# Modulation rows of gate_a, shift_f and scale_f: two weight tiles scaled and summed ahead of one TensorE pass

## Chip, cores and metric

The kernel runs on one core of one Trainium2 chip. The metric is device time in microseconds (us), the median of several executions; lower is better.

## What is computed

Two transformer blocks run one after the other on 256 tokens of width 2048, in float32. The part that matters here is the modulation of the first block: one vector `c` of 2048 numbers becomes six vectors of 2048.

```
mod = silu(c) @ w_ada[l] + b_ada[l]            # w_ada: 2048 x 12288
shift_a, scale_a, gate_a, shift_f, scale_f, gate_f = split(mod, 6)
h = rms_norm(x, g_attn_pre) * (1 + scale_a) + shift_a
proj = h @ w_in                                 # then two kinds of attention
x = x + gate_a * rms_norm(concat(diff_out, dsa_out) @ w_o, g_attn_post)
h = rms_norm(x, g_ffn_pre) * (1 + scale_f) + shift_f
x = x + gate_f * rms_norm((silu(h @ w_gate) * (h @ w_up)) @ w_down, g_ffn_post)
```

The second block (latent attention and a gated convolution) follows and has nothing of this modulation.

## The kernel before

Every engine has one queue, executed in the order in which the program emits. A driver in Python, `run`, writes that order out by hand. Its input is a list of steps. A matmul step takes a unit of 2 x 128 rows of a weight matrix by up to 512 columns. Each unit is split first: ScalarE copies it to a rounded part `wh` (L286), VectorE subtracts to get the rest `wl` (L287), and TensorE then multiplies high by high, low by high and high by low (three matmuls `mm` for each 128 rows and 128 tokens). Splits are emitted up to three units ahead of the matmuls (`LOOK = 3`), into four buffers each (`N_SPLIT = 4`).

Weights arrive as tiles of 128 x 2048 numbers (1 MB) in a ring of four buffers `raw`, and two or three more (`rawb`) lent from other storage. SyncE (SP) issues their transfers in the order of the list, each when a buffer has been released.

A modulation step (`ada`) has a tile of its own in the same ring: 128 rows of `w_ada` by the 2048 columns of one of the six vectors. Before, `ada_full` gives each tile straight to TensorE: a column of silu(c), repeated to 32 columns, is the stationary side, and four float32 products of 512 columns go side by side to four strips of 32 columns of the array, summed in one PSUM bank over 16 tiles. The trace shows eight instructions for the four products. After the sixteenth tile a finishing generator is spawned: `col_fin` for shift_f and scale_f, `row_fin` for gate_a.

The 32 steps of gate_a and shift_f are merged evenly among the matmul steps of the second part of w_in (`sd`), the 16 steps of scale_f among those of the first half of w_o (`so1`). Both attentions run in the background of these steps as generators (`idx_gen`, `dsa_gen`, `diff_gen`): each yields a time, and the driver resumes it when its own clock, which counts matmul columns, has passed it. `softmax_stage` does the row maximum on VectorE (L871) and the exponentials on ScalarE (L877), VectorE scales the result (L927, L989, L990), and TensorE transposes it (`tp<-ident,p`). `gate_f` comes later and keeps `ada_full`; of its tiles eleven are already scaled and summed by VectorE into `adacc` (L660).

Of the kernel before, what the change touches and what calls it, by code (L numbers as in the profile page):

```python
# [9 lines left out]
F32 = mybir.dt.float32  # L10
# [3 lines left out]
AF = mybir.ActivationFunctionType  # L14
OP = mybir.AluOpType
AX = mybir.AxisListType

P = 128
D = 2048
# [20 lines left out]
def kernel(ctx: ExitStack, tc: tile.TileContext, a, freq, out):  # L40
    nc = tc.nc
# [13 lines left out]
    V, A, G = nc.vector, nc.scalar, nc.gpsimd  # L55
# [15 lines left out]

    T = PE

    # ------------------------------------------------------------------ storage
    slots = deque(range(14))
    slot_of = {}

# [8 lines left out]
    def free(*names):  # L86
        for n in names:
            slots.append(slot_of.pop(n))
# [30 lines left out]
    def sc_bank():  # L119
        return psx.tile([P, 512], F32, name="sc", tag="sc", bufs=2)  # L120

    # ------------------------------------------------------------------ driver
    bg = []
    H = {}

# [9 lines left out]
    def spawn(gen, name=None):  # L135
        h = Handle()
        if name is not None:
            H[name] = h
        e = [gen, clock["t"], h]
        if step_gen(e):  # L140
            bg.append(e)
        return h
# [73 lines left out]
    def release(it):  # L216
        ring.append(it["res"])
        lend(lent["max"])

    def run(steps):  # L220
# [74 lines left out]
        for s in steps:  # L295
            if s["kind"] == "call":
                s["fn"]()
                continue
            if s["kind"] == "ada":
                s["item"]["use"](s["item"]["tile"])  # L300
                s["item"]["left"] = 0
                release(s["item"])
                s["after"]()
                pump_dma()
                pump_split(max(0, first_open))
                tick()
                continue
            u, ts = s["unit"], s["ts"]
            g = u["grp"]
            if g.need is not None:  # L310
                names = [x for t in ts for x in g.need(u["kcs"], t)]
                if not done(*names):
                    require(names, g.name)
                    keep_warm(g, ts[0])
            while pos["split"] <= u["idx"]:
                n0 = pos["split"]
                pump_dma()
                pump_split(u["idx"])
                assert pos["split"] > n0, g.name
            for i, kc in enumerate(u["kcs"]):  # L320
                for t in ts:
                    if t not in g.ps:
                        g.ps[t] = mm_bank()
                    hi, lo = g.lhs(kc, t)
                    o = g.ps[t][:, :g.n]
                    fs, ls = kc == g.kcs[0], kc == g.kcs[-1]
                    T.matmul(o, hi, u["wh"][:, i, :g.n], start=fs, stop=False)
                    T.matmul(o, hi, u["wl"][:, i, :g.n], start=False, stop=False)
                    T.matmul(o, lo, u["wh"][:, i, :g.n], start=False, stop=ls)
                if i + 1 < len(u["kcs"]):  # L330
                    tick()
            if s["fin"]:
                unit_done[u["idx"]] = True
                while first_open < len(units) and unit_done[first_open]:
                    first_open += 1
            pump_split(u["idx"])
            for t in s["ends"]:
                spawn(g.post(t, g.ps[t][:, :g.n]), f"{g.name}.{t}")
            tick()
# [9 lines left out]
    def merge(xs, ys, frac=1.0):  # L349
        res, j = [], 0  # L350
        nx = max(1, int(frac * len([x for x in xs if x["kind"] == "mm"])))
        i = 0
        for x in xs:
            res.append(x)
            if x["kind"] == "mm":
                i += 1
                while j < len(ys) and (j + 1) * nx <= i * len(ys) + 0:
                    res.append(ys[j])
                    j += 1
        res += ys[j:]  # L360
        return res

# [9 lines left out]
                t = tt  # L372
            stages[-j](items[i])

    # ------------------------------------------------------------------ constants
    v1 = wtile(tag="P", bufs=4, name="v1")
    v1 = v1[:, :P]
    rows = lambda v, n: v.rearrange("o (r c) -> (o r) c", c=P)[:n]
# [125 lines left out]
        V.tensor_scalar(nlam, nlam, 0.2, None, op0=OP.subtract)  # L504


    # ------------------------------------------------------------------ helpers
    def rstd_of(ssq, n, width, name="rstd"):
        k = ssq.shape[1]
        v = small(k, name + "v")  # L510
# [41 lines left out]
            A.activation(h, src, AF.Copy, scale=scale)  # L552
            V.scalar_tensor_tensor(l, src, scale, h, op0=OP.mult, op1=OP.subtract)

    # ------------------------------------------------------------------ modulation
    def ada_item(load, use, after=lambda: None):
        return {"kind": "ada", "item": {"kind": "ada", "load": load, "use": use}, "after": after}

# [41 lines left out]
    def ada_chunk_fin(ci, ps):  # L600
        k0, nk = CH[ci]
        w = nk * P
        sb = wtile(name="adasb")
        A.activation(sb[:, :w], ps[:, :w], AF.Copy)
        yield 3.0
        pb = quad_transpose(sb[:, :w])
        c2_ = small(16, "c2")
        c2 = c2_[:, :2 * nk].rearrange("p (k g) -> p k g", g=2)
        V.tensor_copy(c2, pb[:, :, 0:64:32])
        V.tensor_add(c2, c2, pb[:, :, 64:P:32])  # L610
        V.scalar_tensor_tensor(Acol[:, k0:k0 + nk], c2[:, :, 1], 1.0, col1[:, 64 + k0:64 + k0 + nk],
                               op0=OP.add, op1=OP.add)
        V.tensor_mul(Acol[:, k0:k0 + nk], Acol[:, k0:k0 + nk], col1[:, 16 + k0:16 + k0 + nk])
        V.tensor_add(tcol[:, k0:k0 + nk], c2[:, :, 0], col1[:, 48 + k0:48 + k0 + nk])
        if k0 == 8:
            while len(slots) < 2:
                yield 0.5
            hid["hi"][1], hid["lo"][1] = big("h1h1", dt=R32), big("h1l1", dt=R32)
        for kc in range(k0, k0 + nk, 2):
            tl, j = nT[kc // 8], kc % 8  # L620
            h = hid["hi"][kc // 8][:, j:j + 2, :]
            for d in range(2):
                A.activation(h[:, d, :], tl[:, j + d, :], AF.Identity, scale=Acol[:, kc + d:kc + d + 1],
                             bias=tcol[:, kc + d:kc + d + 1])
                V.tensor_scalar(tl[:, j + d, :], tl[:, j + d, :], Acol[:, kc + d:kc + d + 1],
                                tcol[:, kc + d:kc + d + 1], op0=OP.mult, op1=OP.add)
            V.tensor_sub(hid["lo"][kc // 8][:, j:j + 2, :], tl[:, j:j + 2, :], h)  # L627
            mark(f"h.{kc}")
            yield 0
        if ci == 2:  # L630
            free("nT0")
        if ci == 4:
            free("nT1")

    def ada_full(which, fin, engs="P" * 16):
        st = {}
# [39 lines left out]
    def col_fin(dst, boff, scale_g=None):  # L676
        def gen(ps):
            sb = wtile(name="adasb")
            A.activation(sb, ps, AF.Copy)
            yield 4.13  # L680
            pb = quad_transpose(sb)
            d = dst.rearrange("p (j b) -> p b j", b=4)
            V.tensor_copy(d, pb[:, :, 0:P:32])
            V.tensor_add(dst, dst, col1[:, boff:boff + 16])
            if scale_g is not None:
                V.scalar_tensor_tensor(dst, dst, 1.0, col1[:, scale_g:scale_g + 16], op0=OP.add,
                                       op1=OP.mult)
        return gen
# [28 lines left out]
                set_state("ada_free", True)  # L717
        return gen

    # ------------------------------------------------------------------ first norm  # L720
    ssx = cst.tile([P, 2, 4], F32, name="ssx")
    first = ada_chunk(0)
    firsts = []
# [25 lines left out]
    free("x0", "x1", "ada0", "ada1", "ada2", "ada3")  # L749
    hid["hi"], hid["lo"] = [big("h1h0", dt=R32), None], [big("h1l0", dt=R32), None]  # L750

    # ------------------------------------------------------------------ w_in of the first block
    acc = {}
    for q in range(2):
        acc["A", q] = big(f"accA{q}", (P, 2, 2, 512))
# [39 lines left out]
            s += g.steps()  # L795
        return s

    # index scores and the selection of keys
    iws = cst.tile([P, 2, 16], F32, name="iws")

    def idx_gen():
# [301 lines left out]
    steps.insert(len(steps) - 8, call(lambda: lend(2)))  # L1103
    steps.append(call(start_idx))
    steps += win_groups(S_G, range(12, 16), False, "c4") + [call(start_dsa)]
    gate_a = ada_full(2, row_fin("Ga", 2, "g_attn_post"))
    shift_f = ada_full(3, col_fin(tfcol, 80))
    scale_f = ada_full(4, col_fin(Afcol, 96, 32))
    gate_f = ada_full(5, row_fin("Gf", 5, "g_ffn_post"), "PPPPPVVVVVVVVVVV")
    sd = win_groups(D_G, range(4, 16), False, "d")  # L1110
    nd = [i for i, x in enumerate(sd) if x["unit"]["grp"].c0 == 1536][0]
    sd.insert(nd, call(start_diff))
    steps += merge(sd, gate_a + shift_f)

    # ------------------------------------------------------------------ output of the attention
    mix_hi = lambda kc, t: (hid["mh%d" % (kc // 8)][:, kc % 8, t * P:(t + 1) * P],
                            hid["ml%d" % (kc // 8)][:, kc % 8, t * P:(t + 1) * P])
    w_o = a["w_o"][0]
# [91 lines left out]
    def after_o():  # L1210
        free("mh0", "ml0", "mh1", "ml1")

    # ------------------------------------------------------------------ feed-forward
    DFF = 5632
    w_gate, w_up, w_down = a["w_gate"][0], a["w_up"][0], a["w_down"][0]
    lhs2 = lambda kc, t: hilo_lhs(*hid["h2"])(kc, t)
# [103 lines left out]

    steps += fsteps[nf:]

    # ------------------------------------------------------------------ second block
    w_in2 = a["w_in_2"]
    lhs3 = lambda kc, t: hilo_lhs(*hid["h3"])(kc, t)
    need3 = lambda ks, t: [f"h3.{t}.{k // 4}" for k in ks]
# [58 lines left out]
    steps += Grp("ck0", w_in2, 512, 288, range(16), lhs3, post_ck0).steps()  # L1385
    steps += Grp("ck1", w_in2, 800, 288, range(16), lhs3, post_ck1).steps()

    # gated convolution
    C_IN, B_GATE, C_GATE, Z_CONV = 3136, 5184, 7232, 9280
    G_MLA, G_CONV, Z_MLA = 11328, 13376, 1088  # L1390
    uT = {}
# [75 lines left out]
        steps += Grp(f"oconv{g}", a["w_o_conv_2"], 512 * g, 512, range(16), lhs_y, post_oconv(g),  # L1467
                     need=lambda ks, t: [f"bgate{k // 4}.{t}" for k in ks]).steps()

    # latent attention  # L1470
    knT, vt, qnT = [None, None], [None, None], [None, None]

    def kv_alloc():
# [199 lines left out]
    for g in range(4):  # L1673
        steps += Grp(f"omla{g}", a["w_o_mla_2"], 512 * g, 512, range(16), lhs_att, post_omla(g)).steps()

    # output projection
    ot = [None, None]
    x2 = [None, None]
    ssz = cst.tile([P, 2, 4], F32, name="ssz")
# [72 lines left out]
```

## Time and profile before

| | |
|---|---|
| median of 3 runs | 2367.16 us (2366.83 to 2367.84) |
| span of the profiled execution | 2365.9 us |
| its own time beside the span | not listed; the span lies 1.3 us below the median |
| TensorE busy | 2315.8 us, 98% |
| VectorE busy | 1306.1 us, 55% |
| ScalarE busy | 1069.0 us, 45% |
| modulation tiles of gate_a, shift_f, scale_f | 48, used by TensorE from 228.85 to 482 us |

The span goes from the first to the last instruction. PE is TensorE, PEld its weight load, DVE is VectorE, ACT ScalarE, POOL GpSimd, SP SyncE. Matmuls overlap in the records, so a matmul's own duration is longer than the distance from its start to the start of the next one, and it is that distance which counts.

### The profile page before, as it was taken

The page shows a single profiled execution, that of the slowest core. Times are in us where ns is not written, and L with a number is a line of the kernel's source. Part 1 is how long each engine was busy: PE and PEld are TensorE (multiplying, and loading weights), DVE is VectorE, ACT ScalarE, POOL GpSimd, SP SyncE. Part 2 cuts the span into 40 slices and gives each one's busy share as a digit, 9 for nine tenths or more (in the row PEclk, how much of TensorE's full clock was granted, in tenths as well). Part 3 has the DMA queues.
Part 4 walks back from the last instruction along what each step waited for, and adds up shares of the span by engine and source line. Part 5 has one row for each costly group of instructions (what it writes and reads, how often), then busy time and mean ns, then how long its engine had stood idle before and what let it go on. Part 6 is the DMA issues. An engine that isn't in the chain of part 4 may idle for free.

```text
span 2365.9 us, 27898 instructions
## 1 busy us (share of the span) xinstructions
PE 2315.8 (98%) x11044; PEld 1842.3 (78%) x11044; DVE 1306.1 (55%) x1710; ACT 1069.0 (45%) x1503; POOL 96.8 (4%) x117
## 2 busy tenths in 40 slices
PE   7999999999999999999998999999999999999998
PEld 5666666677887888888887888888888988888887
DVE  3656756556664444554556655555544654554554
ACT  4434345546444444434444644444445544444443
POOL 1311011010000000000001000000000000000000
PEclk9999999999999999999999999999999999999999
DMA  9996888957775556556554665565565553565563
GB/s 302 330 320 237 318 309 301 318 209 277 242 261 191 191 192 195 179 196 195 186 188 144 220 195 190 179 200 188 179 204 161 168 171 125 172 219 196 187 204 125
DMA packets 237619, 506.57 MB, mean 214 GB/s; under 512 B 9288, under 2 KB 31984, under 8 KB 228400
## 3 DMA queue, kind: packets, MB, share of 16 engines
q1 hardware_dynamic: 235392, 496.14, 62.3%
q0 software_dynamic: 1872, 8.58, 1.1%
q8 instruction: 86, 1.41, 0.2%
q14 instruction: 45, 0.37, 0.0%
q10 hardware_dynamic: 224, 0.07, 0.0%
HBM read 500.56 MB, written 4.19 MB: 213 GB/s over the span
## 4 chain that ended last, share of the span: by engine, by line
PE 75%; DVE 1%; ACT 1%; issue 1%; POOL 0%; DVEq 0%; POOLq 0%; ACTq 0%
PE mm L65 71%; PE tp L70 1%; PE sc L65 1%; PE tp L65 1%; PE tpb L70 1%; DVE wl L287 0%; DVE xr L1155 0%; ACT h3h L1163 0%; DVE h3l L1166 0%; POOL rstd L513 0%; ACT wh L286 0%; ACT junk L1178 0%; DVE ot L1705 0%; ACT hm L1277 0%; DVE hm L1273 0%
## 5 line engine op out<-in xcount | busy, mean ns | idle before, releaser
L287 DVE TENSOR_TENSOR wl<-raw,wh 128x1024 fp32r<-128x1024 f32 (+3 forms) x723 | 871.9, 1212 | 766.5 <-ACT wh L286 760.4
L286 ACT ACTIVATE wh<-raw 128x1024 fp32r<-128x1024 f32 (+3 forms) x723 | 745.9, 1038 | 696.4 <-PE mm L65 686.3
L65 PE MATMUL mm<-wh,h3h 128*128 128x512 f32 (+1 forms) x992 | 387.1, 390 | 1.7 <-ACT h3h L1163 1.2
L65 PE MATMUL mm<-wl,h3h 128*128 128x512 f32 (+1 forms) x992 | 380.7, 384 | 0.4 <-DVE wl L287 0.4
L65 PE MATMUL mm<-wh,h3l 128*128 128x512 f32 (+1 forms) x992 | 381.0, 384 | 0.0
L65 PE MATMUL mm<-wh,h2h 128*128 128x512 f32 x704 | 276.3, 393 | 0.0
L65 PE MATMUL mm<-wl,h2h 128*128 128x512 f32 x704 | 274.6, 390 | 0.9 <-DVE wl L287 0.9
L65 PE MATMUL mm<-wh,h2l 128*128 128x512 f32 x704 | 274.7, 390 | 0.0
L65 PEld LDWEIGHTS mm<-wh,h3h 128*128 128x128 f32 x992 | 186.7, 188 | 37.8 <-ACT h3h L1163 1.6
L65 PEld LDWEIGHTS mm<-wh,h3l 128*128 128x128 f32 x992 | 186.5, 188 | 37.4 <-DVE h3l L1166 0.4
L65 PEld LDWEIGHTS mm<-wl,h3h 128*128 128x128 f32 x992 | 186.8, 188 | 34.8 <-DVE wl L287 0.6
L65 PE MATMUL mm<-wh,h1h 128*128 128x512 f32 (+2 forms) x384 | 154.0, 401 | 3.4 <-ACT wh L286 2.5
L65 PEld LDWEIGHTS mm<-wl,h2h 128*128 128x128 f32 x704 | 132.5, 188 | 28.1 <-DVE wl L287 1.2
L65 PEld LDWEIGHTS mm<-wh,h2h 128*128 128x128 f32 x704 | 132.5, 188 | 27.7 <-issue 0.8
L65 PEld LDWEIGHTS mm<-wh,h2l 128*128 128x128 f32 x704 | 132.4, 188 | 27.6
L65 PE MATMUL mm<-wl,h1h 128*128 128x512 f32 (+2 forms) x384 | 142.7, 372 | 7.8 <-DVE wl L287 7.8
L65 PE MATMUL mm<-wh,h1l 128*128 128x512 f32 (+2 forms) x384 | 142.0, 370 | 1.9 <-DVE h1l L627 1.9
L65 PE MATMUL mm<-wh,acth 128*128 128x512 f32 x352 | 139.3, 396 | 0.0
L65 PE MATMUL mm<-wh,actl 128*128 128x512 f32 x352 | 137.1, 390 | 0.0
L65 PE MATMUL mm<-wl,acth 128*128 128x512 f32 x352 | 137.0, 389 | 0.0
L65 PEld LDWEIGHTS mm<-wh,h1h 128*128 128x128 f32 x384 | 72.8, 190 | 55.7 <-issue 26.7
L65 PEld LDWEIGHTS mm<-wl,h1h 128*128 128x128 f32 x384 | 72.9, 190 | 21.2 <-DVE wl L287 10.9
(412 smaller groups left out, 2777.7 us busy)
## 6 DMA issues: line engine op xcount, KB each, us to landing
raw<-in_w_in_dram SPq DMA_DIRECT2D x134, 1024.0 KB, 5.2
raw<-in_w_ada_dram SPq DMA_DIRECT2D x47, 1024.0 KB, 4.9
raw<-in_w_gate_dram SPq DMA_DIRECT2D x44, 1024.0 KB, 5.3
raw<-in_w_up_dram SPq DMA_DIRECT2D x44, 1024.0 KB, 5.2
raw<-in_w_down_dram SPq DMA_DIRECT2D x44, 1024.0 KB, 5.1
raw<-in_w_ada_dram SPq DMA_DIRECT2D x36, 512.0 KB, 8.9
rawb<-in_w_ada_dram SPq DMA_DIRECT2D x17, 1024.0 KB, 6.5
raw<-in_w_o_conv_dram SPq DMA_DIRECT2D x16, 1024.0 KB, 5.1
```

What stands on the lines that cost most here:

```text
L65: return nc.tensor.matmul(o, l, r, **kw)
L70: return nc.tensor.transpose(o, i, idn)
L286: A.activation(wh[:, :m, :g.n], src, AF.Copy)
L287: V.tensor_sub(wl[:, :m, :g.n], src, wh[:, :m, :g.n])
```

## The change

A new function `ada_pairs` replaces `ada_full` for gate_a, shift_f and scale_f. The tiles of a vector are taken two by two. ScalarE multiplies the even tile in place by its column of silu(c), in two halves of 1024 columns. VectorE multiplies the odd tile by its own column and adds the even one, again in two halves, in place. Then the even buffer is released. A spawned generator waits 5.0 on the driver's clock, runs four products of the sum with a column of ones on TensorE, and releases the odd buffer. After the eighth pair it goes on to the same finish. `merge` places the odd step directly behind its even one, and `run` leaves the release to the generator.

```
+                if not s.get("keep"):
+                    release(s["item"])
...
+                    if ys[j - 1].get("keep") and j % 2:
+                        res.append(ys[j])
+                        j += 1
...
+    def ada_pairs(which, fin):
...
+        def rows(src, i):
+            if i == 0:
+                st["ps"] = psx.tile([P, 512], F32, name="ada", tag="ada")
+            for j in range(4):
+                T.matmul(st["ps"][32 * j:32 * j + 32, :], ones32, src[:, 512 * j:512 * (j + 1)],
+                         start=i == 0, stop=i == 7, tile_position=(0, 32 * j), skip_group_check=True)
+        def summed(i, item):
+            yield 5.0
+            rows(item["tile"], i)
+            release(item)
+            if i == 7:
+                yield from fin(st["ps"])
+        def even(kc):
+            def use(tl):
+                for j in range(2):
+                    s = slice(1024 * j, 1024 * (j + 1))
+                    A.activation(tl[:, s], tl[:, s], AF.Copy, scale=csil[:, kc:kc + 1])
+                st["one"] = first_item
...
+        def odd(kc):
+            def use(tl):
+                a = st["one"]["tile"]
+                for j in range(2):
+                    s = slice(1024 * j, 1024 * (j + 1))
+                    V.scalar_tensor_tensor(tl[:, s], tl[:, s], csil[:, kc:kc + 1], a[:, s], op0=OP.mult,
+                                           op1=OP.add)
+                release(st["one"])
+            def after():
+                spawn(summed(kc // 2, step["item"]), f"ada{which}" if kc == 15 else None)
...
-    gate_a = ada_full(2, row_fin("Ga", 2, "g_attn_post"))
-    shift_f = ada_full(3, col_fin(tfcol, 80))
-    scale_f = ada_full(4, col_fin(Afcol, 96, 32))
+    gate_a = ada_pairs(2, row_fin("Ga", 2, "g_attn_post"))
+    shift_f = ada_pairs(3, col_fin(tfcol, 80))
+    scale_f = ada_pairs(4, col_fin(Afcol, 96, 32))
```

## Rows read from the trace of the kernel before

**Rows 1.** The page, part 1: busy us, share of the span, instructions of each engine.
```profile
PE 2315.8 (98%) x11044; PEld 1842.3 (78%) x11044; DVE 1306.1 (55%) x1710; ACT 1069.0 (45%) x1503; POOL 96.8 (4%) x117
```
**Rows 2.** The page, part 4: chain that ended last, shares by engine.
```profile
PE 75%; DVE 1%; ACT 1%; issue 1%; POOL 0%; DVEq 0%; POOLq 0%; ACTq 0%
```
**Rows 3.** Instructions of tile ada, 228 to 482 us: count, duration ns min/median/max, starts.
```profile
L65 PE MATMUL ada<-raw,csil x248: 592/604/617, 228.8 to 473.2; 128*32 128x512 f32 x124
L65 PE MATMUL ada<-rawb,csil x136: 592/604/617, 249.3 to 481.6; 128*32 128x512 f32 x136
```
**Rows 4.** Timeline of PE around one modulation tile: start us, duration us, instruction.
```profile
270.64 0.39 PE L65 MATMUL mm<-wl,h1h 128*128 128x512 f32 x1
270.87 0.39 PE L65 MATMUL mm<-wh,h1l 128*128 128x512 f32 x1
271.19 1.06 PE L65 MATMUL ada<-rawb,csil 128*32 128x512 f32 x8
272.18 0.50 PE L65 MATMUL mm<-wh,h1h 128*128 128x512 f32 x1
272.52 0.39 PE L65 MATMUL mm<-wl,h1h 128*128 128x512 f32 x1
```
**Rows 5.** Windows of the stretch with the 48 tiles: busy us (instructions) of each engine.
```profile
228.00:287.00 59.00, 59.00 (x287) 35.73 (x285) 42.52 (x101) 25.33 (x39) 2.61 (x2) 1.00 0.79 293
287.00:330.00 43.00, 43.00 (x225) 27.75 (x228) 25.05 (x56) 17.61 (x46) 5.74 (x9) 1.00 0.90 326
330.00:400.00 70.00, 70.00 (x364) 43.06 (x356) 41.99 (x94) 33.54 (x78) 6.56 (x5) 1.00 0.83 304
400.00:482.00 82.00, 82.00 (x440) 51.30 (x436) 45.04 (x99) 40.43 (x82) 7.10 (x7) 1.00 0.91 327
sum 254.00, PE 254.00 PEld 157.84 DVE 154.60 ACT 116.91 POOL 22.01; mean PE 63.50 PEld 39.46 DVE 38.65 ACT 29.23 POOL 5.50
```
The columns behind the length are PE, PEld, DVE, ACT, POOL, granted clock, DMA share, GB/s.

**Rows 6.** Groups of ACT and DVE, 228 to 482 us; last, tile adacc by itself.
```profile
L286 ACT ACTIVATE wh<-raw 128x1024 fp32r<-128x1024 f32 x34 | 35.3, 1058 | 11.0 <-PE mm L65 9.2 <-DVE wl L287 1.4 <-DMA raw<-in_w_o_dram 0.2
L1041 ACT ACTIVATE mh<-tp,gdiff 128x512 fp32r<-128x512 f32 x4 | 2.7, 686 | 3.8 <-PE tp L70 3.8
L954 ACT ACTIVATE mh<-tp 128x512 fp32r<-128x512 f32 x4 | 2.4, 597 | 3.5 <-PE tp L65 3.5
L287 DVE TENSOR_TENSOR wl<-raw,wh 128x1024 fp32r<-128x1024 f32 x34 | 41.0, 1222 | 30.4 <-ACT wh L286 28.3 <-PE mm L65 2.1
L660 DVE SCALAR_TENSOR_TENSOR adacc<-raw,csil,adacc x10: 2342/2344/2346, 563.9 to 706.0; 128x2048 f32<-128x2048 f32 x10
```
**Rows 7.** Waits of PE, 210 to 500 us: total us, times, longest.
```profile
PE mm L65 <- DVE wl L287: 1.2, 1, 1.2
```
**Rows 8.** Timeline, all engines: the end of one softmax and its transpose.
```profile
447.10 0.48 DVE L990 SCALAR_TENSOR_TENSOR p<-p,rs 128x256 f32<-128x256 f32 x1
...
447.88 1.06 PE L65 MATMUL ada<-raw,csil 128*32 128x512 f32 x8
...
448.87 0.33 PE L70 MATMUL tp<-ident,p 128*128 128x128 f32 x1
```
**Rows 9.** Tenth gate_a tile: its issue, its use; then transfers of its kind, 230 to 400 us.
```profile
260.43 0.33 SPq L642 DMA_DIRECT2D rawb<-in_w_ada_dram  x1
...
280.43 1.06 PE L65 MATMUL ada<-rawb,csil 128*32 128x512 f32 x8
...
rawb<-in_w_ada_dram SPq DMA_DIRECT2D x11, 1024.0 KB, 7.0
```
**Rows 10.** Windows of two slices of 15 us, columns as in Rows 5.
```profile
270.00:285.00 15.00, 15.00 (x80) 8.99 (x78) 14.52 (x49) 4.00 (x5) 1.20 (x1) 1.00 0.89 344
285.00:300.00 15.00, 15.00 (x83) 9.40 (x76) 8.06 (x19) 2.73 (x3) 0.09 (x1) 1.00 1.02 401
```

More of the change, by code (lines that the diff above doesn't have):

```diff
@@ L301, in run @@
                 s["item"]["left"] = 0
-                release(s["item"])
+                if not s.get("keep"):
+                    release(s["item"])
                 s["after"]()
@@ L633, in ada_chunk_fin, with load_of, load @@
             free("nT1")
+    def ada_pairs(which, fin):
+        st = {}
+        def load_of(kc):
+            def load(tl):
+                nc.sync.dma_start(tl, w_ada[kc * P:(kc + 1) * P, which * D:(which + 1) * D])
+            return load
+        def rows(src, i):
[16 more added lines that the diff above has]
+                st["one"] = first_item
+            step = ada_item(load_of(kc), use)
+            first_item = step["item"]
+            step["keep"] = True
+            return step
+        def odd(kc):
[8 more added lines that the diff above has]
+                spawn(summed(kc // 2, step["item"]), f"ada{which}" if kc == 15 else None)
+            step = ada_item(load_of(kc), use, after)
+            step["keep"] = True
+            return step
+        return [(odd if kc % 2 else even)(kc) for kc in range(16)]
     def ada_full(which, fin, engs="P" * 16):
```

## Prediction

> **What bounds the kernel now.** I read the page's first part, then its chain, then windows around the 48 tiles that the change touches, then TensorE's own timeline and its waits there. TensorE is busy 98% of the span [rows 1], and the chain that ended last is three quarters TensorE, with no other engine above 1% [rows 2]. A busy share can hide gaps, because matmuls overlap in the records; so the stretch itself has to be looked at. From 228 to 482 us TensorE never shows an idle moment, at a granted clock of 1.00, which is the 2.4 GHz level [rows 5], and from 210 to 500 us it waited for another engine's data essentially once, 1.2 us for a split [rows 7]. The reader should see that this stretch lasts as long as TensorE's instructions take, and that VectorE (154.6 of 254 us) and ScalarE (116.9) have room on average [rows 5], not everywhere: one slice of 15 us has VectorE at 14.5 [rows 10].
>
> **What the change removes.** 384 instructions, eight for each tile, are the 48 passes [rows 3]. What a pass costs is the time by which it pushes two matmuls apart, not its 1.06 us. Consecutive matmuls start 0.23 us apart (270.64, 270.87); with a pass between them the matmul starting at 270.87 and the second one behind the pass, at 272.52, are 1.65 apart instead of two steps of 0.23 [rows 4]. A pass costs 1.65 - 0.46 = 1.19 us. One pass in two goes: 24 x 1.19 = 28.6 us. The passes that stay have the same shape, with ones as the stationary side, and I take the same price for them. Part of the 1.19 is not streaming: the first gap is 0.32 and the step behind the pass 0.34 instead of 0.23 [rows 4], 0.20 together. The Trainium skill's page "TensorEngine Tiling (Array Packing)", section "Key Properties", says that changing the tiling mode drains the array; by that rule and these rows alike the removed pass takes its two switches with it, whereas pricing the bare pass (0.99) would give 23.8 us.
>
> **What it adds on ScalarE.** Two in-place copies of 128x1024 for each pair, scaled by a column. No such instruction is in the trace. The copy without a column takes 1.058 us, and a column as the scale costs 0.686 - 0.597 = 0.089 at 128x512 [rows 6]. I take 1.15; 48 x 1.15 = 55 us. With 116.9 already there, 172 us in a stretch that would shrink to 225.4: 76%.
>
> **What it adds on VectorE.** Two instructions of 128x1024 for each pair, multiply and add. Half of the 128x2048 form is 1.172, and the subtract of 128x1024 takes 1.222 [rows 6]; the fixed part argues for the second. 48 x 1.22 = 58.6 us. With 154.6 there, 213 us in 225.4: 95%. By stages, where 12, 7, 13 and 16 tiles are used now (6, 3.5, 6.5 and 8 pairs, 2.44 us of VectorE and 1.19 us saved for each): 42.5 + 14.6 = 57.1 in 51.9 us; 25.1 + 8.5 = 33.6 in 38.8; 42.0 + 15.9 = 57.9 in 62.3; 45.0 + 19.5 = 64.5 in 72.5 [rows 5]. In the first stage, the scoring and selection of keys, VectorE would have 5.2 us more work than TensorE leaves time.
>
> **What of this reaches TensorE.** Nothing would if the cover held. The cover is the emission of splits up to three units ahead of the matmuls: a slice with VectorE at 97% shows TensorE fully busy [rows 10], so a short overload is absorbed. Three places can lose it.
>
> First, both engines take their queues in order, and behind a pair's work stand the softmax instructions of the attention. There the cover is thin: VectorE finished a p at 447.58 and TensorE used it at 448.87 [rows 8], 1.3 us. A pair puts 2.44 us into VectorE's queue and 2.3 into ScalarE's. A chain with one of them in front is late by up to 2.44 - 1.3 = 1.1 us, by as much again if both are in front, and not at all if they fall between chains. 24 softmax iterations (8 in `dsa_gen`, 16 in `diff_gen`) run behind roughly half of the last three stages, with some 10 of the 18 pairs. I take 1.05 us for each: 10.5 us. Bounds: 0 (every pair falls between) and 10 x 2.2 = 22.
>
> Second, the 5.2 us of overload in the first stage. The lead of the splits absorbs part of it, and the second stage has room to catch up; I take half, 2.6; bounds 0 and 5.2.
>
> Third, the new pass waits for its sum. It is emitted 5.0 on the driver's clock behind the odd step. That clock counts 0.213 us for each matmul of 512 columns; 5.0 is 23.4 of them, 5.4 us at 0.23 [rows 4]. Two copies and the last addition need 1.15 + 1.15 + 1.22 = 3.5 us once ScalarE begins. So 1.9 us are left for whatever is queued ahead. I take 0.05 us for each, 1.2 altogether; the bounds are 0 and the last rival's price.
>
> **Costed at nothing.** The tiles stay in the ring longer and the odd one is wanted half a cycle sooner (a pair in 10.6 us, 254 / 24, so 5.3). The cover: the tenth tile was issued at 260.43 and used at 280.43, 20.0 us for a transfer that lands in 7.0 [rows 9], so 13.0 us of lead. The odd tile's later release costs some 5.4, the earlier use 5.3, and about 2 are left. If that cover is gone, each pair waits on ScalarE for its tile, and the splits behind it are late next. The rate must rise: 79.4 MB in 254 us (from the four rates) become 352 GB/s in 225.4; 401 were reached in a slice [rows 5, 10]. The page "DMA: Bandwidth & Descriptors", section "Specifications", of the Trainium skill gives about 358 GB/s from HBM for a core. The slice at 401 contradicts it as a hard limit here; by the page the last stage, 26.8 MB, could not go below 74.9 us, and the sum would be 2.4 us less good. The finishing generators come later by 5.0 and a little; their consumers are the second half of w_o and the norm behind it, whose 16 units of twelve matmuls take 44 us, so nothing is put down.
>
> **The sum.** 28.6 - 10.5 - 2.6 - 1.2 = 14.3 us. On the profiled span 2365.9 - 14.3 = 2351.6; the median lies 1.3 above that span, which gives 2352.9, say 2353. About 0.2%, 4.7 us, is what a measurement of this kernel can tell from no change.
>
> **Rivals.** *The cover holds* (chance 0.18). TensorE's stretch simply shortens; for it speaks the slice with VectorE at 97% and no wait. Up to 7 us lost: 2367.2 - 28.6 = 2338.6 to 2346. Against it stand the 95% of VectorE.
>
> *VectorE becomes the bound* (0.14). Its 213 us are not filled without gaps: it now idles 30.4 us before 34 subtracts, almost all for ScalarE [rows 6]. If some 30 us of such gaps stay, the stretch takes 213 + 30 = 243, 11 saved; with 40, one us. I put this rival at 2362 to 2372; against it, that a backlog fills gaps.
>
> *Slower* (0.16): each new pass holds TensorE. It has 1.9 us to spare for the queues ahead. ScalarE's copies stand behind a split that waits for a matmul, and VectorE's sums behind that split's subtract (1.22) and whatever softmax or selection is queued. TensorE must lose 28.6 / 24 = 1.19 us at each pass to cancel the gain, which is a lag of 3.1; from 28.6 + 4.7 = 33.3, or 1.4 each, it is slower. A lag of 4.0 gives 24 x 2.1 = 50.4: 2389. For it: 95% on VectorE makes lags of several us likely; against: TensorE's wait lets VectorE catch up, so the lag limits itself. The Trainium skill's "TensorE: Matmul & The Clock Gate", Part 1, calls the queues of ScalarE and VectorE strictly first in, first out; by that rule there is no way past a pair that waits, which is this rival's condition.
>
> **How the numbers follow.** The forecast, some of the gain given back (0.52), has 2346 to 2362 as its own range. Faster: 0.52 + 0.18 + 0.02 of the bound case = 0.72. Same: 0.12. Slower: 0.16. The range goes from 2339, nothing lost, to 2367, where VectorE eats everything: it leaves out the slower case and a part of the bound case, about 2 in 10.
>
> **What would show it.** After: 192 instructions on tile ada in this stretch instead of 384; scaled copies near 1.15 and sums near 1.22; VectorE at 85 to 95%; TensorE waiting for transposes of p and at the new passes, some 14 us altogether; stages two to four shorter, the first nearly not. From the norm behind w_o on, both traces should run alike, shifted. Wrong would be: no waits on TensorE (the first rival), waits at each pass above 1.2 us (the last), or SP transfers landing after their use.

## The result and the profile after

The changed kernel takes 2423.15 us (median of 4 runs, 2421.93 to 2424.87) against 2367.5 before (the three runs of the first table and a fourth): a ratio of 1.0238, with a 95% interval of 1.0223 to 1.0252. It is 55.7 us slower. The forecast was 2353 and faster, with 0.16 for slower; the time lies outside the range. The profiled execution took 2424.2 us and its span is 2422.5.

The page's first part (busy us, share, instructions) and the chain's shares, which answer to [rows 1] and [rows 2]:

```profile
PE 2319.9 (96%) x10864; PEld 1846.4 (76%) x10864; DVE 1361.3 (56%) x1758; ACT 1116.6 (46%) x1551; POOL 96.5 (4%) x117
PE 85%; DVE 6%; ACT 3%; issue 3%; DMA 2%; POOL 0%; SPq 0%; DVEq 0%; POOLq 0%; ACTq 0%
```

VectorE and ScalarE are on the chain now, with 6% and 3%, and even transfers are, with 2%. TensorE's busy share fell from 98% to 96%: it waits.

The instructions of tile ada that belong to the pairs, with their count and first and last start, as [rows 3]:

```profile
L65 PE MATMUL ada<-raw,ones x128: 592/605/972, 235.7 to 510.7; 128*32 128x512 f32 x128
L65 PE MATMUL ada<-rawb,ones x64: 592/605/617, 322.1 to 499.4; 128*32 128x512 f32 x64
```

The change does what it says: 192 instructions where 384 were. But the last pass starts near 510 us, not at 481. The windows of that stretch, of what follows it, and the sum, with the columns of [rows 5]:

```profile
228.00:510.00 282.00, 241.36 (x1063) 153.49 (x1061) 194.00 (x345) 152.13 (x257) 18.74 (x18) 0.98 0.73 267
510.00:539.00 29.00, 18.32 (x75) 10.82 (x73) 17.24 (x58) 13.89 (x38) 3.12 (x4) 0.76 0.34 121
```

Before, 254 us held the 48 tiles with no gap on TensorE. Now 282 us hold 24 passes, with 41 us in which the record shows TensorE idle; then 29 us follow, from 510 to 539, in which it holds 75 instructions and the transfers run at 121 GB/s. VectorE is busy 194 of 282 us, 69%, far from the 95% of my sum: no engine is full in this stretch. The new instructions have nearly the prices that I gave them, as the groups of ScalarE and VectorE from 228 to 512 us show (behind the bar: busy us, mean ns of one, idle before):

```profile
L665 ACT ACTIVATE raw<-raw,csil 128x1024 f32<-128x1024 f32 x38 | 41.5, 1144 | 2.3 <-DMA raw<-in_w_ada_dram 2.3
L286 ACT ACTIVATE wh<-rawb 128x1024 fp32r<-128x1024 f32 x28 | 29.2, 1054 | 12.2 <-DMA rawb<-in_w_in_dram 12.2
L677 DVE SCALAR_TENSOR_TENSOR raw<-raw,csil 128x1024 f32<-128x1024 f32 x24 | 30.7, 1321 | 1.9 <-ACT raw L665 1.9
L677 DVE SCALAR_TENSOR_TENSOR rawb<-rawb,csil,raw 128x1024 f32<-128x1024 f32 x14 | 17.3, 1279 | 0.3 <-ACT raw L665 0.3
```

1.144 us against 1.15, and about 1.28 against 1.22 (one long instance raises the first mean). The splits beside them take what they took before, 1.05 for a copy and 1.22 to 1.23 for a subtract, so they have not become slower either. The error is not in the price of an instruction. Where TensorE waits, from 225 to 560 us (total us, times, longest), against the single 1.2 us of [rows 7]:

```profile
PE mm L65 <- DVE wl L287: 24.6, 26, 3.4
PE tp L70 <- DVE osb L1084: 5.9, 2, 3.8
PE mm L65 <- ACT wh L286: 3.9, 6, 2.3
...
PE ada L65 <- DVE rawb L677: 2.1, 1, 2.1
...
PE ada L65 <- DVE raw L677: 1.1, 1, 1.1
```

The largest of these waits is for the splits, not for the new passes. (What a pass loses once it has begun is not in these rows; e4 shows it.) One such place in the timeline of the changed kernel:

```profile
361.43 1.07 ACT L286 ACTIVATE wh<-rawb 128x1024 fp32r<-128x1024 f32 x1
...
362.54 1.23 DVE L287 TENSOR_TENSOR wl<-rawb,wh 128x1024 fp32r<-128x1024 f32 x1 [0.68 <-ACT wh L286]
...
362.56 0.49 PE L65 MATMUL mm<-wh,h1h 128*128 128x512 f32 x1 [2.26 <-ACT wh L286]
...
363.82 0.80 PE L65 MATMUL mm<-wl,h1h 128*128 128x512 f32 x1 [0.77 <-DVE wl L287]
```

TensorE takes `wh` as soon as ScalarE has written it and `wl` as soon as VectorE has: the split is just in time, with no lead. The order in which the two programs emit shows why. It can be counted from the kernels themselves, since the driver runs when a program is built. At each of the 72 matmul steps of this stretch one to four units were split, the step's own included: one, two, three and four at 3, 20, 24 and 25 steps before, and at 34, 38, none and none after. The driver holds a split back until its clock has passed the modelled landing of its tile, unless it is for the step at hand or the next, and that clock counts TensorE's columns: with 24 passes fewer it runs 20.5 us less while the modelled transfers stay the same. By its clock no modulation tile was used before its modelled landing in the kernel before, 39 of 48 after.

The 29 us behind the stretch, on TensorE:

```profile
520.76 1.12 PE L70 MATMUL tp<-ident,p 128*128 128x128 f32 x4 [1.46 <-ACT osb L1070]
524.04 1.08 PE L70 MATMUL tp<-ident,osb 128*128 128x128 f32 x4 [2.17 <-DVE osb L1084]
...
526.82 3.78 PE L65 MATMUL tp<-accV,pt 128*128 128x128 f32 x16 [0.47 <-ACT pt L1055]
534.37 1.09 PE L70 MATMUL tp<-ident,osb 128*128 128x128 f32 x4 [3.77 <-DVE osb L1084]
535.25 3.99 PE L347 MATMUL mm<-caus,negi 128*128 128x512 bf16 x12
538.89 0.58 PE L65 MATMUL mm<-wh,mh 128*128 128x512 f32 x1
```

This is the end of the attention, step after step with no matmul of weights between, and then the twelve warming matmuls that the driver emits where a group had to wait. The second half of w_o needs the attention; before, it was finished in time, since the attention's generators are paced by the same clock. From here on both kernels take the same: 2365.9 - 482 = 1884 us before and 2422.5 - 539 = 1884 after. In the experiments that follow, all but e3, this rest lies between 1881.5 and 1885.8, so nearly all that they differ in lies before it.

### The profile page after: what moved, and what is told of

It is laid out like the page before. It is cut to its first block, busy times and chain, and to the rows that moved or that the text cites. A ratio compares the mean times of both kernels' runs of the same rounds, so it can differ in the third digit from the quotient of the medians.

```text
span 2422.5 us, 27651 instructions
## 1 busy us (share of the span) xinstructions
PE 2319.9 (96%) x10864; PEld 1846.4 (76%) x10864; DVE 1361.3 (56%) x1758; ACT 1116.6 (46%) x1551; POOL 96.5 (4%) x117
## 4 chain that ended last, share of the span: by engine, by line
PE 85%; DVE 6%; ACT 3%; issue 3%; DMA 2%; POOL 0%; SPq 0%; DVEq 0%; POOLq 0%; ACTq 0%
PE mm L65 78%; DVE wl L287 2%; PE ada L65 2%; PE tp L70 2%; PE sc L65 1%; ACT wh L286 1%; PE tp L65 1%; DVE raw L677 1%; ACT raw L665 1%; DVE rawb L677 1%; PE tpb L70 1%; ACT p L930 0%; DMA raw<-in_w_in_dram 0%; DMA raw<-in_w_o_dram 0%; DVE nm L924 0%
## 5 line engine op out<-in xcount | busy, mean ns | idle before, releaser
L287 DVE TENSOR_TENSOR wl<-raw,wh 128x1024 fp32r<-128x1024 f32 (+3 forms) x715 | 862.4, 1211 | 775.6 <-ACT wh L286 771.8
L286 ACT ACTIVATE wh<-raw 128x1024 fp32r<-128x1024 f32 (+3 forms) x715 | 737.8, 1038 | 687.7 <-PE mm L65 678.5
```

Of the source, the lines that this page charges most:

```text
L286: A.activation(wh[:, :m, :g.n], src, AF.Copy)
L287: V.tensor_sub(wl[:, :m, :g.n], src, wh[:, :m, :g.n])
```

## The experiments

Two theories stood at the start. *Load*: the added work on ScalarE and VectorE, as the prediction had it, only larger. *Clock*: the passes that are gone were counted by the driver's clock, so splits lose their lead and the attention its cover. Each ratio is to the kernel before, with its 95% interval; a line of three dots stands for code left out.

**e1, fewer passes.** The kernel before, with half the passes gone and nothing in their place:

```
-                if engs[kc] == "P":
-                    rows(crep(kc), tl, kc == firstp, kc == 15 and not away)
+                if engs[kc] == "P" and not away:
+                    if kc % 2 == 0:
+                        rows(crep(kc), tl, kc == 0, kc == 14)
```

> The kernel before with the passes of the 24 odd tiles left out (their numbers are missing from the three vectors); no copies, no sums, every buffer released as before. Theory L (load: the added work on ScalarE and VectorE is what costs): nothing is added here, so the full 28.6 us are gained, 2339. Theory K (clock: the driver's clock no longer counts 24 x 0.85 = 20.5 us of passes, so splits are emitted closer to their use and the attention in the background is not finished when the second half of w_o needs it, and its rest runs without cover): the second half of w_o waits for some 20 us of attention, so the gain is 15 at most, 2352 to 2370, with the twelve warming matmuls of keep_warm (L346) in the trace ahead of w_o's second half.

Measured 2371.95, ratio 1.0019 (1.0010 to 1.0029), 2 us above the range that *clock* had. Taking 28.6 us of work from an engine that is busy 98% of the time, and adding none elsewhere, made the kernel 4.5 us slower. *Load* cannot explain that. The expected sign is in its timeline on TensorE:

```profile
471.79 1.09 PE L70 MATMUL tp<-ident,osb 128*128 128x128 f32 x4 [2.15 <-DVE osb L1034]
...
474.60 3.62 PE L65 MATMUL tp<-accV,pt 128*128 128x128 f32 x16 [0.47 <-ACT pt L1005]
481.98 1.08 PE L70 MATMUL tp<-ident,osb 128*128 128x128 f32 x4 [3.77 <-DVE osb L1034]
482.86 3.69 PE L346 MATMUL mm<-caus,negi 128*128 128x512 bf16 x12
```

The attention's end is bare here as well, with the warming matmuls behind it, and no step of the stretch has four units split (one, two and three at 15, 56 and 1).

**e2, no load.** The changed kernel without the two loops of ScalarE and VectorE:

```
-                    A.activation(tl[:, s], tl[:, s], AF.Copy, scale=csil[:, kc:kc + 1])
...
-                    V.scalar_tensor_tensor(tl[:, s], tl[:, s], csil[:, kc:kc + 1], a[:, s], op0=OP.mult,
-                                           op1=OP.add)
```

> The changed kernel without the scaled copies on ScalarE and the sums on VectorE (the pass multiplies the odd tile as it was loaded, so the vectors are wrong); pairs, holding of buffers, the wait of 5.0 and the order of everything else are the changed kernel's. Theory L: nearly all of the loss goes away, and TensorE's saving shows: 2340 to 2355. Theory K: the emission is the same as after, so the loss of cover stays; the uncovered attention of some 28 us ahead of w_o's second half stays in the trace, 2375 to 2410.

Measured 2386.61, ratio 1.0079 (1.0064 to 1.0094), within the range of *clock*. Both theories are half right: 36.5 us go with the load, and 19.2 us of loss remain without it. The bare end stays in the trace: behind the last weight matmuls of w_o's first half TensorE has only attention, the last passes and the warming matmuls for 29 us.

**e3, no gate.** Splits are no longer held back:

```
-                if u["item"]["due"] > clock["t"] and i > cur + NEAR:
-                    return
```

> The changed kernel without the rule that holds a split back until the driver's clock has passed the modelled landing of its tile (two lines of pump_split; it holds for the whole kernel). Splits are then emitted three to four units ahead in the stretch, not one to two. If the short lead of the splits is the larger part of the loss, 20 to 40 us come back: 2385 to 2403. If tiles really land late, ScalarE's queue waits for them at the head and little comes back: 2410 to 2440. Theory L has no reason for a change: 2423.

Measured 2470.62, ratio 1.0432 (1.0417 to 1.0448): 47 us worse than the change and above all three ranges. Three or four units were split at every step of the stretch. ScalarE's waits in it, from 228 to 580 us, say why:

```profile
ACT wh L284 <- DMA raw<-in_w_in_dram: 41.7, 7, 11.8
ACT wh L284 <- DMA raw<-in_w_o_dram: 22.7, 5, 6.6
ACT wh L284 <- DMA rawb<-in_w_in_dram: 12.9, 2, 11.0
```

Splits emitted early stand at the head of ScalarE's queue until their tile has landed, 77 us in these three rows, and whatever stands behind them waits too. So the tiles of w_in and w_o are really late for early splits: the rule that shortens the lead guards against something that is there. (The rule is off in the whole kernel in this run, but that is not where the loss comes from: up to the stretch the run is 8.7 us ahead of the changed kernel, behind it 8.6 slower, and the stretch itself takes 48.6 us more.)

**e4, old clock.** One line in the odd step puts the missing columns back on the driver's clock:

```
             def use(tl):
+                clock["t"] += 2048 * 4.0 / 2400.0 * 0.25
                 a = st["one"]["tile"]
```

> The changed kernel with the driver's clock advanced by the 0.85 us of the left-out pass at each odd tile, so that its pace per matmul step is the old one; no instruction is added or left out, only the order of emission moves. Theory K: the splits get their lead back (one to four units), modelled landings come before use at 46 of 48 tiles, and w_o's second half waits for some 11 instead of 33 us on the driver's clock; most of the 56 us return: 2360 to 2385. Theory L: the same load stands in the same queues, 2410 to 2425.

Measured 2399.82, ratio 1.0133 (1.0117 to 1.0148). No instruction is added or left out, and 23.3 us are gone. The time falls between the two expectations, which agrees with e2. Its timeline has the warming matmuls at 510.39, 0.7 us behind the start of the last attention transposes:

```profile
509.73 0.82 PE L70 MATMUL tp<-ident,osb 128*128 128x128 f32 x4 [1.28 <-DVE osb L1085]
510.39 4.44 PE L347 MATMUL mm<-caus,negi 128*128 128x512 bf16 x12
```

So the old order is not quite back: one, two, three and four units were split at 11, 24, 29 and 8 steps, between the two kernels, and a short bare end is left, 12.5 us from the last weight matmul of w_o's first half to the first of its second, against 34.2 in the changed kernel.

The trace also shows what a late sum does to a pass. A pass begins when the first half of its sum is done, and here its last four weight loads wait 1.05 us for the second half:

```profile
375.25 0.14 PEld L65 LDWEIGHTS ada<-raw,ones 128*32 128x32 f32 x4 [1.90 <-DVE raw L678]
375.25 2.25 PE L65 MATMUL ada<-raw,ones 128*32 128x512 f32 x8 [1.47 <-DVE raw L678]
...
376.45 0.14 PEld L65 LDWEIGHTS ada<-raw,ones 128*32 128x32 f32 x4 [1.05 <-DVE raw L678]
```

The four strips no longer start together, and the pass takes 2.25 us instead of 1.06 [rows 4], all of it counted as busy. Eight of the 24 passes take more than 1.2 us from their start to the next instruction instead of 0.99, 7.9 us over all; with the 3.2 us of waits ahead of passes that is 11 us here, and 9.8 (6.5 and 3.2) in the changed kernel. Without sums (e2, e6, e8) no pass is longer.

**e5, fewer passes with the old clock.** e1 with that line in the branch that leaves a pass out.

```
+                    else:
+                        clock["t"] += 2048 * 4.0 / 2400.0 * 0.25
```

> The kernel before with the 24 odd passes left out, as in e1, but the driver's clock advanced by 0.85 us for each, so that every other instruction stands where it stood in the kernel before. Theory K says that e1 lost its 28.6 us to the moved emission alone: with the old order most of it comes back, 2338 to 2350. If the attention's own chain of engines or the transfers set the length of the stretch, the old order helps little: 2355 to 2372.

Measured 2346.77, ratio 0.9915 (0.9900 to 0.9930): 20.6 us faster. That is what the removed passes are worth when everything else stays in its place, and e1 lost all of it, 25.2 us, to the clock alone.

TensorE's instructions come in the same order here as in the kernel before, so the two timelines can be lined up one by one. At 23 of the 24 places the removed pass closes the gap by 1.08 to 1.20 us, at one a wait takes its place; together 27.1. Elsewhere 6.1 us are given back, 4.2 of them at one place, a wait for an attention result with matmuls at half the pace behind it:

```profile
377.68 0.40 PE L65 MATMUL mm<-wh,h1l 128*128 128x512 f32 x1
380.61 0.69 PE L70 MATMUL tp<-ident,p 128*128 128x128 f32 x2 [2.54 <-ACT osb L1022]
380.96 0.78 PE L65 MATMUL mm<-wh,h1h 128*128 128x512 f32 x1
381.53 0.63 PE L65 MATMUL mm<-wl,h1h 128*128 128x512 f32 x1
381.96 0.63 PE L65 MATMUL mm<-wh,h1l 128*128 128x512 f32 x1
```

**e6, no load with the old clock** (the edits of e2 and e4 together):

```
             def use(tl):
+                clock["t"] += 2048 * 4.0 / 2400.0 * 0.25
                 release(st["one"])
```

> The changed kernel without copies and sums, with the driver's clock advanced by the left-out pass (e2 and e4 together). Against e4 it prices the work on ScalarE and VectorE with the better order, against e5 the pairing and the longer holding of the buffers. From e4 (2400) and the 36 us between after and e2: 2360 to 2368, if the two causes add. If the load only hurts where cover is short, the load's share is smaller here: 2370 to 2390.

Measured 2358.33, ratio 0.9966 (0.9951 to 0.9980), 1.7 below the expected span. Against e4, the load costs 41.5, with the same order of emission. Against e5, pairing and holding cost 11.6 us. That is not holding alone: the order of emission is that of e4, not that of e5, which emits as the kernel before does. So the warming matmuls stand here too, and e5 has none of them:

```profile
470.15 0.83 PE L70 MATMUL tp<-ident,osb 128*128 128x128 f32 x4 [1.28 <-DVE osb L1077]
470.81 2.75 PE L347 MATMUL mm<-caus,negi 128*128 128x512 bf16 x12
473.22 0.58 PE L65 MATMUL mm<-wh,mh 128*128 128x512 f32 x1
```

**e7, steps apart.** e4 without the edit of `merge`:

```
-                    if ys[j - 1].get("keep") and j % 2:
-                        res.append(ys[j])
-                        j += 1
```

> e4 with the odd step left at its own even place in the list (the edit of merge undone), so ScalarE's copies and VectorE's sums come some 5 us apart and the odd tile is wanted that much later; the even buffer is held longer instead. If the burst of two steps and the earlier need of the odd tile carry part of the loss: 2375 to 2393. If only the amount of work counts: 2395 to 2402.

Measured 2394.33, ratio 1.0116 (1.0101 to 1.0131): 5.5 us better than e4, between the two expectations. The place of the odd step matters, but little; and moving it changes the order of emission as well (one to four units at 5, 28, 24 and 15 steps), so the 5.5 are not the burst's alone.

**e8, no sums.** e4 without VectorE's loop, ScalarE's kept:

```
-                    V.scalar_tensor_tensor(tl[:, s], tl[:, s], csil[:, kc:kc + 1], a[:, s], op0=OP.mult,
-                                           op1=OP.add)
```

> e4 without VectorE's sums, with ScalarE's copies kept (the pass multiplies the odd tile as loaded, so the vectors are wrong). If VectorE, the fuller of the two, carries the price of the load, this comes near e6: within 8 us of it. If ScalarE's copies at the head of its queue, waiting for their tile, carry it, this stays within 8 us of e4's 2400.

Measured 2371.94, ratio 1.0021 (1.0011 to 1.0030). Neither: 13.6 us above e6, 27.9 below e4.

**e12, no copies.** e4 without ScalarE's loop, VectorE's kept:

```
-                    A.activation(tl[:, s], tl[:, s], AF.Copy, scale=csil[:, kc:kc + 1])
```

> e4 without ScalarE's copies, with VectorE's sums kept (the even tile is added unscaled, so the vectors are wrong). With e6 (neither, 2358.3), e8 (copies alone, 2371.9) and e4 (both, 2399.8) it fills the table. If the two loads add, sums alone cost 27.9: 2386. If VectorE's sums hurt mainly because they wait at the head of its queue for the copies: 2365 to 2376.

Measured 2380.25, ratio 1.0060 (1.0044 to 1.0077), between the two expectations. With e6, e8 and e4 the table is: neither 2358.3, copies 2371.9 (+13.6), sums 2380.3 (+21.9), both 2399.8 (+41.5). The two add up to 35.5 of the 41.5; 6.0 come from having both.

The waits of TensorE from 225 to 560 us in e6 and then in e4:

```profile
PE mm L65 <- DVE wl L287: 4.6, 7, 0.8
```
```profile
PE mm L65 <- DVE wl L287: 9.3, 10, 3.6
PE tp L65 <- ACT pt L1056: 5.3, 4, 2.6
...
PE sc L65 <- ACT p L931: 3.3, 4, 1.3
PE ada L65 <- DVE raw L678: 3.2, 3, 1.5
```

With the load, TensorE waits longer for splits, for both attentions' results and for the sums; none of them dominates. The sums' share is larger than their row, since most of it lies within the passes: 11 us, as e4 showed.

**e10 and e11, pairs for one vector only**, with the old clock. e10 keeps them for shift_f, as below; e11 keeps them for scale_f and sets gate_a and shift_f back:

```
-    gate_a = ada_pairs(2, row_fin("Ga", 2, "g_attn_post"))
+    gate_a = ada_full(2, row_fin("Ga", 2, "g_attn_post"))
...
-    scale_f = ada_pairs(4, col_fin(Afcol, 96, 32))
+    scale_f = ada_full(4, col_fin(Afcol, 96, 32))
```

> e4 with pairs for shift_f alone (8 pairs, between some 320 and 400 us); gate_a and scale_f as before. If each pair costs what the 24 of e4 cost on average, (2399.8 - 2367.4) / 24 = 1.35 us, it is 8 x 1.35 = 10.8 slower: 2378. If the pairs only cost because they follow so closely that cover never recovers, a third of them does much less than a third of the harm: 2362 to 2371.

> e4 with pairs for scale_f alone (8 pairs, between some 400 and 482 us, under the first half of w_o, where a tile is wanted most often). By the average of 1.35 us for each pair 2378. If this stage, with VectorE at 89% by my sum, is no worse than the first with 110%: 2368 to 2376; if the density of tiles decides: 2380 or more.

Measured 2375.37, ratio 1.0037 (1.0024 to 1.0051), and 2381.72, ratio 1.0062 (1.0047 to 1.0077). Eight pairs cost 8.8 and 15.1 us, net of the passes that they save, so each vector's pairs lose time by themselves, and of these two stages the one in which tiles are wanted most often is the dearer. It is not the first stage, where I had put VectorE's overload: what is left for gate_a, if the three add up to e4's 32.4, is 8.5.

**e13, no load, apart.** e6 without the edit of `merge`, as in e7:

```
-                    if ys[j - 1].get("keep") and j % 2:
-                        res.append(ys[j])
-                        j += 1
```

> e6 (no copies, no sums, old clock) with the odd step left at its own even place in the list. Against e5 (2346.8) it prices the longer holding of the two buffers, against e6 (2358.3) the earlier need of the odd tile. If the 11.6 us between them are the earlier need: 2346 to 2351. If they are the holding: 2355 to 2360.

Measured 2356.76, ratio 0.9955 (0.9939 to 0.9972). The earlier need of the odd tile is worth 1.6 us without the load; 10.0 of the 11.6 us come with the way by which buffers are held and the pass is put off. The two of these were not told apart, and the warming matmuls are here too, 2.4 us from the first of them to the weight matmul behind.

No run that computes all of the modulation was faster than the kernel before.

## Why the prediction was wrong

The ladder from the kernel before to the changed one, each step the difference of two medians (2367.4, 2346.8, 2358.3, 2399.8, 2423.15):

| step | forecast us | measured us | runs |
|---|---|---|---|
| 24 passes removed | -28.6 | -20.6 | e5 against before |
| pairing, holding, later pass | 0 | +11.6 | e6 against e5 |
| copies and sums | +14.3 | +41.5 | e4 against e6 |
| driver's clock slower | not seen | +23.3 | after against e4 |
| together | -14.3 | +55.8 | |

The miss of 70 us (2423 against 2353) has four parts: 8.0 less gained from the passes, 11.6, 41.5 - 14.3 = 27.2 and 23.3. The split depends on the order of the steps: without the load the clock costs 28.3 (e2 against e6), and with the slower clock the load costs 36.5 (after against e2).

**What bounds the kernel.** Right as long as the order of emission is kept, which the change does not do. The 1.19 us of a pass was right: e5 has 27.1 of the 28.6 us at the places of the passes. 20.6 show in the time, since 6.1 us come back elsewhere, most of it as one wait for an attention result and the slow matmuls behind it. So TensorE's work did set the length of the stretch, but splits, transfers and attention had been laid under it with little to spare.

**The step that failed** is "What of this reaches TensorE": it took the emission of splits up to three units ahead as given. The removed passes are part of what paces that emission. In my third place I converted the wait of 5.0 by the driver's clock, and did not go on to ask what else it paces. It paces the modelled landings against which splits are held back, and the attention's generators. e4 shows its price with the load, 23.3; e1 against e5 without, 25.2; e2 against e6, 28.3. That e1 and the changed kernel both have the bare end of the attention, and e4 hardly, shows one part of it; the shorter lead of the splits is in the order of emission and in the waits for `wl`, 24.6 against 9.3 in e4. The bare end alone is 21.7 us shorter in e4, but some of its work then stands earlier in the stretch, so how the 23.3 divide between the two was not measured.

**Costed at nothing.** The holding of the tiles was covered, I said, by 13.0 us of lead at the tenth tile, of which about 2 would be left. With the later pass it cost 10 to 12 us without any load (e6, e13), of which 2.4 are warming matmuls, so a part of this step is the driver's order of emission once more. The lead of a modulation tile was the wrong cover to look at: ScalarE waited for them hardly at all after the change either, 2.3 us in its row. Late are the weight tiles behind them in the same ring, whose splits have to wait: 12.2 us in the changed kernel, 14.9 in e6 and 15.0 in e13 against 5.2 in e5 (ScalarE's waits for transfers within the stretch), and 77 in e3. That the held buffers make them late was not tested by itself.

**The load.** The term of the sum was mis-sized: 14.3 forecast with bounds of 0 to 27.2 for its first two places, 41.5 measured. Instruction prices were right within 5%. The third place is the one whose size can be read directly: 1.2 forecast, 9.8 us measured at the new passes, 3.2 ahead of them and 6.5 within them, where I had no row for a pass whose sum comes in two halves. The first place was priced at ten pairs, each with one short delay, and the second at the first stage alone; e10 and e11 show loss in each of the other two vectors, most under w_o. That both engines' work adds up (13.6, 21.9, and 6.0 for both) fits two queues in which everything behind a pair is late; how the rest divides between late splits and late softmax was not separated.

**The rivals.** The one on the slower side had the right sign for another reason: it needed 1.4 us lost at each new pass, and the 9.8 us are 0.4 for each (TensorE's weight loads of these passes waited 10.5 for sums in their rows):

```profile
PEld ada L65 <- DVE raw L677: 5.5, 7, 1.7
...
PEld ada L65 <- DVE rawb L677: 5.0, 4, 2.5
```

Its condition was real all the same: the Trainium skill's page "TensorE: Matmul & The Clock Gate", Part 1, has these queues strictly first in, first out, and e3 agrees as far as its rows go: for 77 us ScalarE did nothing but wait for the tile of the split at its head. VectorE as the bound is refuted by its 69% in the stretch. That the rate of the transfers would not set the time holds: the stretch moved 267 GB/s, less than before; single tiles landed late all the same. The switch of tiling mode, for which I cited the Trainium skill's page "TensorEngine Tiling (Array Packing)", section "Key Properties", was not tested by itself; e5 agrees with the price that I took by it, since at 19 of the 24 places a removed pass takes 1.19 to 1.20 us with it, not the bare 0.99.

Of the signs that I had named, the counts, the prices of the instructions and the like run behind w_o came true. VectorE at 85 to 95%, some 14 us of waits (41 us idle in the stretch alone) and shorter stages did not. Of the signs of being wrong one came, transfers that landed late: those of the weight tiles.

## What to carry to other kernels

In a schedule written by a clock that counts one engine's work, that work is also the ruler: before pricing a removal, ask what is paced by it, and try the removal alone, with the clock kept and with the clock moved (e5 and e1, 25 us apart). An engine that is 98% busy can lose 28.6 us of work and gain nothing, when the removal also moves the order in which everything else is issued. Work moved onto half-idle engines with in-order queues is not free, here 41.5 us for 116 us of work (48 copies of 1.144 and 48 sums of 1.278) on engines that were busy 46 and 61% of the stretch. And a busy share can hide a wait: four products that run side by side are counted as busy for 2.25 us instead of 1.06 when half of their input is late.

## What the runs showed of the hardware

VectorE's multiply-and-add over 128x1024 takes 1.278 us at the median of its instances, more than half of the 2.344 for 128x2048 [rows 6]: two halves cost 0.21 us more than one whole.

TensorE's clock fell behind some of its waits. A window of the changed kernel, with the columns of [rows 5]; then matmuls of one kind in its timeline, behind a wait of 2.81 us and a little later:

```profile
375.00:390.00 15.00, 11.18 (x35) 7.64 (x36) 9.42 (x15) 5.93 (x7) 2.50 (x2) 0.89 0.41 136
```
```profile
384.31 0.80 PE L65 MATMUL mm<-wl,h1h 128*128 128x512 f32 x1 [2.81 <-DVE wl L287]
...
385.33 0.63 PE L65 MATMUL mm<-wh,h1h 128*128 128x512 f32 x1
385.75 0.63 PE L65 MATMUL mm<-wl,h1h 128*128 128x512 f32 x1
...
388.44 0.39 PE L65 MATMUL mm<-wh,h1h 128*128 128x512 f32 x1
388.66 0.39 PE L65 MATMUL mm<-wl,h1h 128*128 128x512 f32 x1
```

Starts are 0.42 apart, the lower of the two levels (1.2 GHz), and 3 us later 0.22. Before, the granted clock was 1.00 through the whole stretch. I had not put this on the bill of a wait, and it is part of the steps of the ladder. It is a small part of them, as far as the weight matmuls show: of the starts of two of them with no wait between, 23 of 512 are 0.38 to 0.46 apart in the changed kernel's stretch and 8 of 526 in that of the kernel before. By 15 more at 0.19 us each I estimate 3 us.
